# SwiGLU block of a two-layer encoder trunk: block products in two PSUM banks, scratch tiles taken out, and loads of the down stretch placed elsewhere

## The chip, the cores and the metric

One core of a Trainium2 chip runs the whole program in one launch. The metric is the device time of that launch in microseconds (us). TensorE (PE in the profile) does matmuls, VectorE (DVE), ScalarE (ACT) and GpSimd (POOL) do elementwise work, and SyncE (SP) issues nearly all DMA transfers from one queue, in order.

## The reference

Two layers work on x of 1024 tokens by 1024 channels in float32. Each layer has a mixing half (windowed attention, spatial gating, a convolution) and then the block that is changed here, followed by a gated projection of a side input p (1024 by 256 for each layer):

```
h = RMSNorm(x) * g_ffn
x = x + (silu(h @ w_gate) * (h @ w_up)) @ w_down        # w_gate_up: 1024 x 5632, w_down: 2816 x 1024
x = x + (p[i] @ w_ple_proj) * sigmoid(RMSNorm(x) @ w_ple_gate)
```

## The kernel before, in words

**Layout and precision.** Activations lie with channels in the 128 partitions and tokens along the free axis, in two halves of 512 tokens (`HALF`, `hf`). Every float32 operand is split in two parts, `wh`/`wl` for weights and the two halves of an `hl` or `tf` tile for activations. One step of a product (`step_mm`, L224, L226, L228) is then three matmuls of 128x128 by 128x512. ScalarE makes the first part of a split (`copy_h`, L122), VectorE the second (`sub_l`, L125 and L216). `load_w` (L211 to L216) loads a weight tile into one of three `raw` slots and splits it into one of three `wh` and three `wl` slots.

**Where tiles live.** `U` gives one of 38 tiles of 1024 floats, `T` one of 6 scratch tiles of 512 floats (tags `s`, `sg`, `ws`, `cu`, `t1`, `u2`, `g`, `ac`, `st`, `sq` and others all share these six). PSUM has eight banks of 128x512: three behind `BA` (`pa`), four behind `BT` (`pt`), one behind `BO` (`po`). `BU` alternates between `BT` and `BA`. The order of the instructions on each engine is not the order of the code: a scheduler in the framework lays them out, and inserts a wait where a slot or a bank has to come free first.

**Gate and up products.** The 2816 inner channels are worked as 11 pairs `j` of 2x128. For a pair, gate (`i`=0) and up (`i`=1) are 2x2 block products over two halves of the 1024 channels, done with seven block products in place of eight. `first(j)` (L1118) does the two block products that belong to token half 0 and the first 128 channels of the pair: for `k`=0..3 into a bank, VectorE saves that partial sum times the norm's row `bc` in `s1` (L1131) which goes to DRAM (`sum_d`, L1132), then `k`=4..7 go on in the same bank, and the finished bank is multiplied (L1137), passed through silu (L1138), multiplied on GpSimd (L1139), and for up multiplied into the result (L1141), which goes to `act_d`. `rest(j)` (L1172) does the other five products for gate and for up, 60 matmuls each: GpSimd makes sums of weight blocks (L1216 to L1220; the first, `s3`, in a scratch tile `ws`), ScalarE and VectorE split them (`wform`), the products go to three banks, and VectorE adds them up (L1224, L1226) and ends them (`out_of`: L1208 and silu L1209 for gate; L1212 into a scratch tile `cu` and then L1213 for up). The results go to `act_d` (L1233, L1234).

**Order.** `first(0)` to `first(4)` run while the mixing half still runs (the ahead stage; there all banks come from `BA` and the weight parts are cast on VectorE, L215, and subtracted on GpSimd). Then the second token half is finished (`wo_second(1)`), `token_forms` (L1156) normalises x (`normed`, L1153) and makes the token sums and their splits, `first(5)` to `first(7)` follow (with the forms: the token-form stage), then `rest(0)` to `rest(10)`, with one of `first(8)` to `first(10)` behind each of `rest(0)` to `rest(2)`. From `rest(3)` on no first is left; these are called steady rests here.

**Down stretch.** The side input p is loaded into `raw` slots and transposed (L1262, L1267), `w_ple_proj` as well (L1275). Then for each token half: x is loaded (L1285), and for the 22 tiles of 128 inner channels a `w_down` tile (L211) and an activation tile `ac` in a scratch slot (L1291) are loaded, split, and multiplied into all eight banks; L1299 adds x and `norm_add` starts the next norm.

## Time and profile before

| | us |
|---|---|
| median of 3 runs | 2665.69 |
| lowest and highest of them | 2662.81, 2669.3 |
| the profiled execution | 2667.72 |
| its span in the trace | 2665.9 |
| mean granted clock of TensorE | 0.952 of full speed |

The profile is one execution, 2.0 us slower than the median. Times in rows count from the start of the span. "Idle before" is how long the engine stood still before an instruction, with the instruction that released it. The rows are of layer 1; layer 2 has the same sequence.

### The profile page before, as it was taken

The page shows a single profiled execution, that of the slowest core. Times are in us where ns is not written, and L with a number is a line of the kernel's source. Part 1 is how long each engine was busy: PE and PEld are TensorE (multiplying, and loading weights), DVE is VectorE, ACT ScalarE, POOL GpSimd, SP SyncE. Part 2 cuts the span into 40 slices and gives each one's busy share as a digit, 9 for nine tenths or more (in the row PEclk, how much of TensorE's full clock was granted, in tenths as well). Part 3 has the DMA queues.
Part 4 walks back from the last instruction along what each step waited for, and adds up shares of the span by engine and source line. Part 5 has one row for each costly group of instructions (what it writes and reads, how often), then busy time and mean ns, then how long its engine had stood idle before and what let it go on. Part 6 is the DMA issues. An engine that isn't in the chain of part 4 may idle for free. (4 is left out here: it accounts for less than half of the span.)

```text
span 2665.9 us, 30234 instructions
## 1 busy us (share of the span) xinstructions
PE 2387.9 (90%) x11404; PEld 1972.8 (74%) x11404; DVE 1453.5 (55%) x2241; ACT 905.5 (34%) x1610; POOL 744.6 (28%) x551
## 2 busy tenths in 40 slices
PE   8898889688988889899999898896898888898999
PEld 6897767567766668688789876675776666786887
DVE  6986674644544452525469567646444444526252
ACT  5246661312222241424323457412212222424142
POOL 5123345532332300103421233464323333001031
PEclk9999998899999989899999999898999999999999
DMA  6011324333333262523321031344333332625332
GB/s 205 24 52 56 119 84 161 118 124 113 131 103 103 87 217 95 198 95 107 96 71 37 33 111 64 126 150 123 123 111 99 103 103 87 241 95 197 95 99 67
DMA packets 243346, 294.78 MB, mean 111 GB/s; under 512 B 11348, under 2 KB 180912, under 8 KB 243200
## 3 DMA queue, kind: packets, MB, share of 16 engines
q1 hardware_dynamic: 236704, 283.16, 32.4%
q10 hardware_dynamic: 6016, 9.45, 1.1%
q8 instruction: 90, 1.47, 0.2%
q0 software_dynamic: 480, 0.24, 0.1%
q14 instruction: 56, 0.46, 0.1%
HBM read 228.84 MB, written 63.96 MB: 110 GB/s over the span
## 5 line engine op out<-in xcount | busy, mean ns | idle before, releaser
L216 DVE TENSOR_TENSOR wl<-raw,wh 128x1024 fp32r<-128x1024 f32 x172 | 218.9, 1273 | 337.5 <-ACT wh L122 327.7
L224 PE MATMUL pt<-tf,wh 128*128 128x512 f32 x792 | 326.5, 415 | 54.7 <-ACT wh L122 54.7
L122 ACT ACTIVATE wh<-raw 128x1024 fp32r<-128x1024 f32 x172 | 182.0, 1059 | 532.2 <-PE pt L226 376.9
L226 PE MATMUL pt<-tf,wh 128*128 128x512 f32 x792 | 323.3, 408 | 0.0
L224 PE MATMUL pa<-hl,wh 128*128 128x512 f32 x648 | 264.4, 409 | 62.9 <-DVE s L1131 52.9
L228 PE MATMUL pt<-tf,wl 128*128 128x512 f32 x792 | 315.4, 404 | 0.0
L224 PE MATMUL pa<-tf,wh 128*128 128x512 f32 x704 | 280.0, 400 | 19.5 <-ACT wh L122 19.5
L264 POOL TENSOR_TENSOR st<-st,sq 128x512 f32<-128x512 f32 x82 | 123.4, 1506 | 610.2 <-ACT sq L263 607.9
L228 PE MATMUL pa<-tf,wl 128*128 128x512 f32 x704 | 273.1, 394 | 9.2 <-DVE wl L125 9.2
L226 PE MATMUL pa<-tf,wh 128*128 128x512 f32 x704 | 277.0, 394 | 0.0
L228 PE MATMUL pa<-hl,wl 128*128 128x512 f32 x648 | 259.1, 404 | 4.5 <-POOL wl L216 3.3
L226 PE MATMUL pa<-hl,wh 128*128 128x512 f32 x648 | 262.1, 405 | 1.0 <-DVE hl L128 0.8
L224 PEld LDWEIGHTS pt<-tf,wh 128*128 128x128 f32 x792 | 159.4, 201 | 98.4 <-ACT wh L122 64.0
L1216 POOL TENSOR_TENSOR ws<-rw,rw 128x512 f32<-128x512 f32 x44 | 63.7, 1448 | 511.5 <-DVE cu L1212 337.6
L224 PEld LDWEIGHTS pa<-hl,wh 128*128 128x128 f32 x648 | 125.8, 194 | 99.6 <-DVE s L1131 59.3
L607 PE MATMUL pa<-wh,hl 128*128 128x256 f32 x640 | 181.1, 288 | 16.4 <-ACT zkv L620 11.7
L226 PEld LDWEIGHTS pt<-tf,wh 128*128 128x128 f32 x792 | 157.6, 199 | 33.9
L228 PEld LDWEIGHTS pt<-tf,wl 128*128 128x128 f32 x792 | 156.3, 197 | 34.2
L609 PE MATMUL pa<-wl,hl 128*128 128x256 f32 x640 | 181.6, 286 | 0.0
L610 PE MATMUL pa<-wh,hl 128*128 128x256 f32 x640 | 180.8, 286 | 0.0
L224 PEld LDWEIGHTS pa<-tf,wh 128*128 128x128 f32 x704 | 134.9, 192 | 55.7 <-ACT wh L122 28.8
L122 ACT ACTIVATE wh<-rw 128x512 fp32r<-128x512 f32 x176 | 102.6, 618 | 208.2 <-POOL rw L1218 172.8
(309 smaller groups left out, 4933.9 us busy)
## 6 DMA issues: line engine op xcount, KB each, us to landing
rw<-in_w_gate_up_dram SPq DMA_DIRECT2D x88, 512.0 KB, 6.0
raw<-in_w_down_dram SPq DMA_DIRECT2D x88, 512.0 KB, 3.6
raw<-in_w_gate_up_dram SPq DMA_DIRECT2D x44, 512.0 KB, 4.5
ac<-act SPq DMA_DIRECT2D x88, 256.0 KB, 5.0
raw<-in_w_ple_gate_dram SPq DMA_DIRECT2D x32, 512.0 KB, 4.1
raw<-in_w_in_dram SPq DMA_DIRECT2D x28, 512.0 KB, 3.8
raw<-in_w_out_dram SPq DMA_DIRECT2D x24, 512.0 KB, 3.7
sum<-s SPq DMA_DIRECT2D x44, 256.0 KB, 2.2
```

The source lines that it names most:

```text
L122: nc.scalar.activation(dst, src, AF.Copy, scale=scale)
L216: (eng or nc.vector).tensor_tensor(out=l, in0=raw, in1=f(h), op=ALU.subtract)
L224: nc.tensor.matmul(b, lhsT=wh, rhs=hl[:, 0:512], start=first, stop=False, skip_group_check=again)
L226: nc.tensor.matmul(b, lhsT=wh, rhs=hl[:, 512:1024], start=False, stop=False, skip_group_check=again)
L228: nc.tensor.matmul(b, lhsT=wl, rhs=hl[:, 0:512], start=False, stop=last, skip_group_check=again)
L264: (eng or nc.gpsimd).tensor_tensor(out=n.s, in0=n.s, in1=sq, op=ALU.add)
L607: nc.tensor.matmul(o, lhsT=x_[:, th], rhs=wh, start=(kc + k == 0), stop=False)
L609: nc.tensor.matmul(o, lhsT=x_[:, th], rhs=wl, start=False, stop=False)
L610: nc.tensor.matmul(o, lhsT=x_[:, tl], rhs=wh, start=False, stop=(kc == 1 and k == 3))
L1216: tt(out=s3, in0=a21, in1=a22, op=ALU.add)
```

## The change

In `first`, both weight tiles are loaded ahead of the products, and each product's two halves go to two banks instead of one (from `BA` in the ahead stage, otherwise from `BU`). The first bank gives `s1` (L1137 of the changed kernel), the second is multiplied by `bc` in place, in PSUM (L1140), `s1` is added (L1141), and silu (L1143) and the product of gate and up (L1144) follow; the multiply on GpSimd is gone. In `rest`, the weight sum `s3` takes the free half of the result tile `ga`, and the tile `cu` is replaced by work in place in the bank (L1213, L1214) or in `g` (L1231, L1232). p is loaded early into `U` tiles, `w_ple_proj` during tile 8 and x during tile 12 of the down stretch, and `ac` takes a `U` tile.

```diff
--- before.py
+++ after.py
@@ -1119,27 +1119,30 @@
 
             hl0, bc = nrm[0].hl, nrm[0].bc
             c0 = 2 * j * P
-            a = None
-            for i, off in enumerate((0, DFF)):
-                wh, wl = load_w(rows_of(w_gate_up[layer], 0, NK, off + c0, P), (NK, P),
-                                nc.gpsimd if ahead else None, nc.vector if ahead else None)
-                b = BA()
-                for k in range(NK):
-                    step_mm(b, (wh[:, k, :], wl[:, k, :]), hl0[k], k == 0, k % HK == HK - 1, True)
-                    if k == HK - 1:
-                        s1 = T("s1")
+            ws = [load_w(rows_of(w_gate_up[layer], 0, NK, off + c0, P), (NK, P),
+                         nc.gpsimd if ahead else None, nc.vector if ahead else None)
+                  for off in (0, DFF)]
+            a = T("sg")
+            for i, (wh, wl) in enumerate(ws):
+                bank = BA if ahead else BU
+                s1 = T("s1")
+                for h in range(2):
+                    b = bank()
+                    for k in range(h * HK, (h + 1) * HK):
+                        step_mm(b, (wh[:, k, :], wl[:, k, :]), hl0[k], k % HK == 0,
+                                k % HK == HK - 1)
+                        if k % 2 == 1:
+                            bg.tick()
+                    if h == 0:
                         nc.vector.tensor_tensor(out=s1, in0=b, in1=bc, op=ALU.mult)
                         nc.sync.dma_start(out=sum_d[j][i], in_=s1)
-                    if k % 2 == 1:
-                        bg.tick()
+                    else:
+                        nc.vector.tensor_tensor(out=b, in0=b, in1=bc, op=ALU.mult)
+                        nc.vector.tensor_tensor(out=b if i else a, in0=b, in1=s1, op=ALU.add)
                 if i == 0:
-                    a = T("sg")
-                    nc.vector.tensor_tensor(out=a, in0=b, in1=bc, op=ALU.mult)
                     nc.scalar.activation(a, a, AF.Silu)
-                    nc.gpsimd.tensor_tensor(out=a, in0=a, in1=bc, op=ALU.mult)
-                else:
-                    nc.vector.tensor_tensor(out=a, in0=b, in1=a, op=ALU.mult)
-                    nc.sync.dma_start(out=act_d[2 * j][:, HALF[0]], in_=a)
+            nc.vector.tensor_tensor(out=a, in0=b, in1=a, op=ALU.mult)
+            nc.sync.dma_start(out=act_d[2 * j][:, HALF[0]], in_=a)
 
         forms = [[None] * HK for _ in range(5)]
 
@@ -1182,8 +1185,7 @@
                                                               off + 2 * j * P, 2 * P))
                 a11, a21, a12, a22 = (raw[h][:, :, c * P:(c + 1) * P] for h in range(2)
                                       for c in range(2))
-                sm = T("ws")
-                s3 = sm.rearrange("p (k m) -> p k m", k=HK)
+                s3 = ga[:, 0:512].rearrange("p (k m) -> p k m", k=HK)
                 tt = nc.gpsimd.tensor_tensor
                 pool_w = []
 
@@ -1208,13 +1210,11 @@
                         nc.vector.tensor_tensor(out=dst, in0=b, in1=src, op=ALU.add)
                         nc.scalar.activation(dst, dst, AF.Silu)
                     else:
-                        c = T("cu")
-                        nc.vector.tensor_tensor(out=c, in0=b, in1=src, op=ALU.add)
-                        nc.vector.tensor_tensor(out=dst, in0=c, in1=dst, op=ALU.mult)
+                        nc.vector.tensor_tensor(out=b, in0=b, in1=src, op=ALU.add)
+                        nc.vector.tensor_tensor(out=dst, in0=b, in1=dst, op=ALU.mult)
 
                 bank = BT if i else BA
                 tt(out=s3, in0=a21, in1=a22, op=ALU.add)
-                w22 = None
                 tt(out=a21, in0=a11, in1=a21, op=ALU.subtract)
                 tt(out=a11, in0=s3, in1=a11, op=ALU.subtract)
                 tt(out=a12, in0=a12, in1=a11, op=ALU.subtract)
@@ -1225,7 +1225,12 @@
                 prod(bd, wform(a21), 1, True, True)
                 nc.vector.tensor_tensor(out=g, in0=bd, in1=u2, op=ALU.add)
                 prod(bc_, wform(s3), 2, True, True)
-                out_of(gb[:, 512:1024], g, bc_)
+                if i == 0:
+                    out_of(gb[:, 512:1024], g, bc_)
+                else:
+                    nc.vector.tensor_tensor(out=g, in0=bc_, in1=g, op=ALU.add)
+                    nc.vector.tensor_tensor(out=gb[:, 512:1024], in0=g, in1=gb[:, 512:1024],
+                                            op=ALU.mult)
                 prod(bd, wform(a22), 3, False, True)
                 out_of(gb[:, 0:512], u2, bd)
                 prod(bc_, wform(a12), 4, False, True)
@@ -1255,44 +1260,50 @@
                 first(AHEAD + 1 + BEHIND + j)
 
 
+        pin = [U("pin").rearrange("p (b m) -> p b m", b=4) for _ in range(2)]
+        for hf in range(2):
+            nc.sync.dma_start(out=pin[hf], in_=p[layer, 0, hf * 512:(hf + 1) * 512, :]
+                              .rearrange("(b q) m -> q b m", q=P))
...
         pw = []
-        for c in range(2):
-            raw = wp.tile([P, 1024], F32, tag="raw", name=nm("praw"))
-            nc.sync.dma_start(out=raw, in_=w_ple_proj[layer, c * P:(c + 1) * P, :])
-            ph, pl = U("pwh", F32R), U("pwl", F32R)
-            copy_h(ph, raw)
-            sub_l(pl, raw, ph)
-            pw.append((ph, pl))
+
+        def proj_weights():
+            for c in range(2):
+                raw = U("praw")
+                nc.sync.dma_start(out=raw, in_=w_ple_proj[layer, c * P:(c + 1) * P, :])
+                ph, pl = U("pwh", F32R), U("pwl", F32R)
+                copy_h(ph, raw)
+                sub_l(pl, raw, ph)
+                pw.append((ph, pl))
+
 
         nx = [None, None]
         for hf in range(2):
-            xps = [U("X").rearrange("p (m s) -> p m s", m=2) for _ in range(4)]
-            for mp in range(4):
-                nc.sync.dma_start(out=xps[mp], in_=xd[2 * mp:2 * mp + 2, :, HALF[hf]]
-                                  .rearrange("m p s -> p m s"))
             banks = [BO()] + [BA() for _ in range(3)] + [BT() for _ in range(4)]
             for fi in range(NF):
                 wh, wl = load_w(rows_of(w_down[layer], fi * P, 1, 0, D), (1, D))
-                t = T("ac")
+                t = U("ac")[:, 0:512]
                 nc.sync.dma_start(out=t, in_=act_d[fi][:, HALF[hf]])
                 a = split(t)
                 for m in range(NK):
                     cs = slice(m * P, (m + 1) * P)
                     step_mm(banks[m], (wh[:, 0, cs], wl[:, 0, cs]), a, fi == 0, fi == NF - 1)
+                if fi == 8 and hf == 0:
+                    proj_weights()
+                if fi == 12:
+                    xps = [U("X").rearrange("p (m s) -> p m s", m=2) for _ in range(4)]
+                    for mp in range(4):
+                        nc.sync.dma_start(out=xps[mp], in_=xd[2 * mp:2 * mp + 2, :, HALF[hf]]
+                                          .rearrange("m p s -> p m s"))
             nx[hf] = Norm()
             for m in range(NK):
                 xo = X[hf][m] = xps[m // 2][:, m % 2]
```

**VectorE in the ahead stage of layer 1**, where the row `st_2511` of the first norm becomes known (`pa` are the banks of the firsts, X the tiles of x that L1153 or L1156 normalise). Before, behind L1131 for `pa_4065` and seven of the eight L1153:

```order
L1153 SCALAR_TENSOR_TENSOR X_3790<-X_3790,cols_189,st_2511 128x512
L215 CAST wh_4172<-raw_4171 128x1024
L1137 TENSOR_TENSOR sg_4093<-pa_4065,st_2511 128x512
L1131 TENSOR_TENSOR s_680_4116<-pa_4103,st_2511 128x512
L1131 TENSOR_TENSOR s_685_4152<-pa_4139,st_2511 128x512
L215 CAST wh_4208<-raw_4207 128x1024
L1141 TENSOR_TENSOR sg_4093<-pa_4103,sg_4093 128x512
```

Now, behind L1137 for `pa_4073`, four of the eight L1156 and a cast:

```order
L1156 SCALAR_TENSOR_TENSOR X_3788<-X_3788,cols_189,st_2511 128x512
L1140 TENSOR_TENSOR pa_4088<-pa_4088,st_2511 128x512
L1156 SCALAR_TENSOR_TENSOR X_3790<-X_3790,cols_189,st_2511 128x512
L1156 SCALAR_TENSOR_TENSOR X_3788<-X_3788,cols_189,st_2511 128x512
L1156 SCALAR_TENSOR_TENSOR X_3790<-X_3790,cols_189,st_2511 128x512
L215 CAST wh_4216<-raw_4215 128x1024
L1140 TENSOR_TENSOR pa_4120<-pa_4120,st_2511 128x512
L1141 TENSOR_TENSOR sg_4071<-pa_4088,s_677_4072 128x512
L1137 TENSOR_TENSOR s_680_4104<-pa_4105,st_2511 128x512
L1141 TENSOR_TENSOR pa_4120<-pa_4120,s_680_4104 128x512
```

The banks' evacuations went from three in a row behind the eighth normalisation to five, spread between normalisations and casts; the bank `pa_4088` comes free with the L1141 near the end of this piece.

**GpSimd in the steady rests** (`rw` are the weight blocks of one `i`; the lower-numbered pair of `rw` is loaded first). Before, the up part of one pair and the gate of the next:

```order
L1216 TENSOR_TENSOR ws_6297<-rw_6293,rw_6294 128x512
L1218 TENSOR_TENSOR rw_6293<-rw_6293 128x4x128
L1219 TENSOR_TENSOR rw_6293<-ws_6297,rw_6293 128x4x128
L1220 TENSOR_TENSOR rw_6294<-rw_6294,rw_6293 128x4x128
L1216 TENSOR_TENSOR ws_6404<-rw_6400,rw_6401 128x512
L1218 TENSOR_TENSOR rw_6400<-rw_6400 128x4x128
L1219 TENSOR_TENSOR rw_6400<-ws_6404,rw_6400 128x4x128
L1220 TENSOR_TENSOR rw_6401<-rw_6401,rw_6400 128x4x128
```

Now, the same two parts:

```order
L1217 TENSOR_TENSOR ga_6208<-rw_6311,rw_6312 128x512
L1218 TENSOR_TENSOR rw_6311<-rw_6311 128x4x128
L1219 TENSOR_TENSOR rw_6311<-ga_6208,rw_6311 128x4x128
L1217 TENSOR_TENSOR ga_6410<-rw_6414,rw_6415 128x512
L1220 TENSOR_TENSOR rw_6312<-rw_6312,rw_6311 128x4x128
L1218 TENSOR_TENSOR rw_6414<-rw_6414 128x4x128
L1219 TENSOR_TENSOR rw_6414<-ga_6410,rw_6414 128x4x128
L1220 TENSOR_TENSOR rw_6415<-rw_6415,rw_6414 128x4x128
```

The first weight sum of the next gate (into `ga_6410`) stands ahead of the last one of the running up part; the sum goes to `ga`, not to a scratch tile `ws`.

TensorE at the same place (`pt` are the banks of the up part, `pa` those of the next gate). Before, the gate's first matmuls stand behind the fifth, last up product:

```order
L226 MATMUL pt_5890<-tf_4707,wh_5961 128x512
L228 MATMUL pt_5890<-tf_4707,wl_5962 128x512
L224 MATMUL pa_5995<-tf_4622,wh_5998 128x512
L226 MATMUL pa_5995<-tf_4622,wh_5998 128x512
L224 MATMUL pa_5996<-tf_4625,wh_5998 128x512
L226 MATMUL pa_5996<-tf_4625,wh_5998 128x512
```

Now 14 of the gate's 60 matmuls (12 into `pa_6018`, 2 into `pa_6019`) stand behind the third up product, and the fourth and fifth follow them:

```order
L228 MATMUL pt_5917<-tf_4721,wl_5953 128x512
L224 MATMUL pa_6018<-tf_4642,wh_6021 128x512
L226 MATMUL pa_6018<-tf_4642,wh_6021 128x512
L224 MATMUL pa_6019<-tf_4645,wh_6021 128x512
L226 MATMUL pa_6019<-tf_4645,wh_6021 128x512
L228 MATMUL pa_6018<-tf_4642,wl_6022 128x512
L224 MATMUL pa_6018<-tf_4666,wh_6021 128x512
```

Of the gate, 46 matmuls are left behind the last up product.

**SP ahead of the down stretch of layer 1** (`rw` and `act` belong to the last two rests, `ac` and `raw_7...<-in_w_down` to the down stretch). Before:

```order
L1234 DMA act_118<-gb_7225 128x1024
L1291 DMA ac_7501<-act_97 128x512
L211 DMA raw_7495<-in_w_down_dram 128x1024
L1291 DMA ac_7536<-act_98 128x512
L1291 DMA ac_7571<-act_99 128x512
L1233 DMA act_117<-ga_7224 128x512
L1291 DMA ac_7606<-act_100 128x512
L1291 DMA ac_7641<-act_101 128x512
L1285 DMA X_7479<-xd 128x2x512
```

Now:

```order
L1265 DMA pin_7420<-in_p_dram 128x4x256
L1265 DMA pin_7421<-in_p_dram 128x4x256
L1295 DMA ac_7470<-act_97 128x512
L1295 DMA ac_7505<-act_98 128x512
L1295 DMA ac_7540<-act_99 128x512
L211 DMA raw_7569<-in_w_down_dram 128x1024
L1295 DMA ac_7575<-act_100 128x512
L1295 DMA ac_7610<-act_101 128x512
L1295 DMA ac_7645<-act_102 128x512
L1239 DMA act_118<-gb_7219 128x1024
L211 DMA raw_7604<-in_w_down_dram 128x1024
```

Three `w_down` tiles (`raw_7464`, `raw_7499`, `raw_7534`) stand some 65 to 78 places further up in the queue, between the rests, and six `ac` loads ahead of the last rest's results; x is not in this piece any more, and p is where `w_ple_proj` was.

## Rows read from the trace of the kernel before

**Rows 1.** The page's first part: engine, busy time in us (share of the span), instructions.

```profile
PE 2387.9 (90%) x11404; PEld 1972.8 (74%) x11404; DVE 1453.5 (55%) x2241; ACT 905.5 (34%) x1610; POOL 744.6 (28%) x551
```

**Rows 2.** The waits of PE over the whole span: engine, first letters of the tile it was to write, its line, then whom it waited for; us in total, times, longest in us.

```profile
PE pt L224 <- ACT wh L122: 54.7, 22, 2.5
PE pa L224 <- DVE s L1131: 52.9, 14, 10.9
PE po L224 <- ACT tf L122: 31.1, 4, 8.8
```

**Rows 3.** Layer 1 in stretches (us from the span's start): busy us of PE, PEld, DVE, ACT, POOL with the number of instructions, granted clock as a share of full speed, DMA share, GB/s.

```profile
497.00:540.00 43.00, 21.20 (x66) 15.87 (x67) 40.12 (x47) 15.24 (x26) 17.52 (x10) 0.68 0.26 84
552.30:690.00 137.70, 123.79 (x513) 98.99 (x514) 67.67 (x90) 31.42 (x51) 37.69 (x28) 0.96 0.36 117
690.00:957.50 267.50, 236.43 (x965) 187.23 (x964) 126.39 (x182) 57.44 (x102) 83.18 (x60) 0.95 0.29 97
957.50:985.00 27.50, 18.32 (x65) 14.30 (x64) 17.09 (x21) 14.06 (x19) 0.00 (x0) 0.81 1.02 368
```

**Rows 4.** The ahead stage of layer 1 in order of time, PE, ACT and DVE: start us, us, engine, line, operation, tiles, xcount, [idle before <-releaser].

```profile
409.19 0.63 PE L226 MATMUL pa<-hl,wh 128*128 128x512 f32 x1
409.62 0.63 PE L228 MATMUL pa<-hl,wl 128*128 128x512 f32 x1
411.27 1.11 PE L281 MATMUL pt<-ident,rcol 128*128 128x128 f32 x4 [0.17 <-POOL rcol L270]
420.36 0.50 PE L224 MATMUL pa<-hl,wh 128*128 128x512 f32 x1 [1.01 <-DVE sg L1137]
...
412.42 0.58 ACT L298 COPY st<-pt 128x512 f32<-128x512 f32 x1 [2.88 <-PE pt L281]
...
413.11 0.69 DVE L1131 TENSOR_TENSOR s<-pa,st 128x512 f32<-128x512 f32 x1 [0.78 <-ACT st L298]
413.72 5.38 DVE L1153 SCALAR_TENSOR_TENSOR X<-X,cols,st 128x512 f32<-128x512 f32 x8
```

**Rows 5.** The token-form stage of layer 1, PE in order of time (columns as in rows 4).

```profile
505.89 0.80 PE L224 MATMUL pa<-hl,wh 128*128 128x512 f32 x1 [9.11 <-DVE s L1131]
548.45 0.50 PE L224 MATMUL pa<-hl,wh 128*128 128x512 f32 x1 [1.38 <-DVE s L1131]
552.31 0.50 PE L224 MATMUL pa<-tf,wh 128*128 128x512 f32 x1 [0.84 <-ACT wh L122]
```

**Rows 6.** One cycle of the steady rests of layer 1 (columns as in rows 4): PE, DVE, ACT, POOL, SP.

```profile
717.80 0.39 PE L228 MATMUL pt<-tf,wl 128*128 128x512 f32 x1
719.12 0.50 PE L224 MATMUL pa<-tf,wh 128*128 128x512 f32 x1 [0.94 <-ACT wh L122]
720.97 0.51 PE L228 MATMUL pa<-tf,wl 128*128 128x512 f32 x1 [0.65 <-DVE wl L125]
721.32 0.40 PE L224 MATMUL pa<-tf,wh 128*128 128x512 f32 x1
733.57 0.39 PE L228 MATMUL pa<-tf,wl 128*128 128x512 f32 x1
736.45 0.50 PE L224 MATMUL pt<-tf,wh 128*128 128x512 f32 x1 [2.49 <-ACT wh L122]
752.92 0.50 PE L224 MATMUL pa<-tf,wh 128*128 128x512 f32 x1 [0.94 <-ACT wh L122]
...
718.23 0.69 DVE L1212 TENSOR_TENSOR cu<-pt,u 128x512 f32<-128x512 f32 x1 [0.96 <-PE pt L228]
718.95 1.36 DVE L1213 TENSOR_TENSOR ga<-cu,ga 128x512 f32<-128x512 f32 x1
...
734.73 0.63 ACT L1209 ACTIVATE ga<-ga 128x512 f32<-128x512 f32 x1 [2.09 <-DVE ga L1208]
...
713.56 1.79 POOL L1216 TENSOR_TENSOR ws<-rw,rw 128x512 f32<-128x512 f32 x1 [13.32 <-DVE cu L1212]
727.94 1.29 POOL L1216 TENSOR_TENSOR ws<-rw,rw 128x512 f32<-128x512 f32 x1 [8.17 <-DMA rw<-in_w_gate_up_dram]
730.68 1.29 POOL L1219 TENSOR_TENSOR rw<-ws,rw 128x512 f32<-128x512 f32 x1
...
720.34 0.32 SPq L1233 DMA_DIRECT2D act<-ga  x1
721.23 2.05 SPq L1181 DMA_DIRECT2D rw<-in_w_gate_up_dram  x4
```

**Rows 7.** The start of the down stretch of layer 1: PE, then SP.

```profile
965.10 0.79 PE L224 MATMUL po<-tf,wh 128*128 128x512 f32 x1 [6.94 <-ACT tf L122]
975.14 0.50 PE L224 MATMUL po<-tf,wh 128*128 128x512 f32 x1 [2.23 <-ACT wh L122]
...
961.31 3.56 SPq L1285 DMA_DIRECT2D X<-xd  x4
965.23 1.65 SPq L211 DMA_DIRECT2D raw<-in_w_down_dram  x3
```

**Rows 8.** The change of halves in the down stretch of layer 1: PE, then ACT.

```profile
1100.12 0.79 PE L224 MATMUL po<-tf,wh 128*128 128x512 f32 x1 [8.83 <-ACT tf L122]
...
1099.43 1.92 ACT L122 ACTIVATE tf<-ac 128x512 fp32r<-128x512 f32 x3 [1.43 <-DMA ac<-act]
```

**Rows 9.** Groups of instructions over the whole span: line, engine, operation, tiles, shapes, xcount | busy us, mean ns of one | idle us before them and releaser.

```profile
L1213 DVE TENSOR_TENSOR ga<-cu,ga 128x512 f32<-128x512 f32 x22 | 29.3, 1332 | 0.5
L1131 DVE TENSOR_TENSOR s<-pa,st 128x512 f32<-128x512 f32 x44 | 29.7, 683 | 17.9 <-PE pa L228 15.7 <-ACT st L298 2.2
L1139 POOL TENSOR_TENSOR sg<-sg,st 128x512 f32<-128x512 f32 x22 | 30.2, 1372 | 55.4 <-ACT sg L1138 46.4 <-issue 9.0
```

8 lines of the change are left out of this document (2 added, 6 removed).

## The prediction, made before the changed kernel ran

> **What bounds the kernel now.** I read the busy times first: TensorE works 2387.9 us of the span, 90% [rows 1]; no other engine is above 55%. A change of the order can therefore only win TensorE's idle time or its time at low clock, and the question is where in the FFN these lie. The waits of TensorE answer it [rows 2]: 52.9 us for L1131, that is for VectorE to read a half-done bank in `first`; 54.7 us for a weight split in `rest`'s up part, 22 times and at most 2.5 us; 31.1 us for an activation split in the down stretch, in four waits. The stretches [rows 3] then say who is behind each wait. From 497 to 540 VectorE is busy 40.1 of 43 us and TensorE 21.2: there VectorE is the bound. In the steady rests (690 to 957.5) TensorE is busy 236 of 267 us and VectorE not half of it, so the idle time is that of a chain. From 957.5 to 985 the DMA engines are full (share 1.02), at 368 GB/s, with a granted clock of 0.81.
>
> Two steps recur. At full clock the sixth and the last of a gate's 60 matmuls start at 721.32 and 733.57 [rows 6]: 54 steps of 0.227 us. At half clock two start 0.43 us apart [rows 4] (409.19 and 409.62). The two levels are 2.4 and 1.2 GHz.
>
> **The change part by part**, for one layer; both layers have the same sequence.
>
> *First, operations.* VectorE did four operations in a `first` and now does seven; with 0.683 us for a product out of PSUM [rows 9] three more are 2.07 us, and over 22 firsts 66 x 0.69 = 45.5 us. GpSimd loses 22 multiplies of 1.37 us, 30.2 us [rows 9], which TensorE never waited for: nothing. Writing into a PSUM bank from VectorE is in no row. The nearest are 0.69 us for PSUM in and SBUF out and 1.33 us for two SBUF operands [rows 9]; I take 0.69, because one operand and the length are the same, and keep 1.33 for the range.
>
> *Ahead stage: +8 us (+4 to +11).* Before, the row `bc` was made by transposes at 411.27, was in SBUF at 413.0, and TensorE began the 49th matmul of the products ahead at 420.36, behind 1.01 us of waiting for L1137 [rows 4]. In the new order the transposes stand behind some 10 matmuls more, at half clock 4.3 us or more: I estimate 415.5 to 417, `bc` ready near 418. TensorE's 49th matmul then needs the bank `pa_4088` (only three `BA` banks take turns). VectorE's order puts ahead of that bank's last read L1137, eight L1156 (5.38 us for eight), two casts, two L1140 and L1141: 0.69 + 5.4 + 1.4 + 1.4 + 0.7, with overlaps some 9.3 us. That is 427.3 in place of 420.36, 7 us, and about 1 us more until the clock is up. Low end: the transposes come first after all. High end: 1.33 us for the work in PSUM.
>
> *Token-form stage: -6 us (-9 to 0).* The waits of 9.1 and up to 10.9 us for L1131 go [rows 2, 5], but VectorE is 93% busy there and gets three firsts more work, 6.2 us. The forms would be done near 540 + 6.2; before, `rest(0)` began at 552.31 after the firsts' left matmuls [rows 5], which in the new order have been done under cover of VectorE's work. So `rest(0)` starts at 546 or so. If VectorE's line of work lengthens all of it, nothing is won.
>
> *Firsts between rests: -6.5 us (-8 to -3).* Each of three has a wait for L1131 of 1.38 us and one of 0.84 us for the next weight split [rows 5]: 2.2 x 3. VectorE, 67.7 busy of 137.7 us [rows 3], covers 2.07 us more.
>
> *Steady rests: -7 us (-15 to +3).* A cycle takes 33.80 us, 719.12 to 752.92, with 120 matmuls (27.2 us), waits of 0.94, 0.65 and 2.49 us, and 2.5 us for the clock and short waits [rows 6]. The first two waits come from GpSimd: L1216 stood 13.32 us for the scratch slot of `cu`, and started the gate's weights only at 713.56. Without the scratch tile they are ready early, and 14 gate matmuls run ahead of the last two up products. The third wait stays, in another form. Before, the up part's weights were ready (L1219 done at 731.97) while ScalarE held their copy behind the silu at 734.73. Now let E be the end of the last up product (before, the matmul at 717.80 ends at 718.2). Only 46 gate matmuls follow, 10.4 us. The up weights' loads are issued by SP behind the `act` write, and that behind L1213: before at 721.23, E + 3.0. With the multiply at 0.69 in place of 1.36 us it is E + 2.4. From issue to L1216 took 6.7 us (727.94), three sums to the end of L1219 take 4.0, ScalarE's copy 0.63: TensorE goes on at about E + 13.8. So a wait of 3.4 us takes the place of all three; then 74 matmuls (16.8 us) and about 2.2 us of low clock and short waits: 32.8 us, 1.0 less, in seven transitions. Best: the wait stays at 2.5 us and the clock falls less. Worst: the multiply takes 1.36 us and the longer wait costs a second stretch at half clock.
>
> The length of that multiply is a row: 1.36 us with two SBUF operands beside GpSimd's work, 0.69 us for the operation out of PSUM [rows 6]. The Trainium skill, page "GPSIMD Engine Reference", section "1. Specifications", says that GpSimd's SBUF interfaces are shared with VectorE, with contention when a VectorE instruction has two SBUF inputs; by it the multiply, with one operand in PSUM now, would not stretch even if GpSimd ran beside it. By the rule the sum stands; by the old row kept, the cycle would be 33.5 us and this term -2 us.
>
> *Start of the down stretch: -12.5 us (-13.3 to -9).* Of 957.5 to 985, 27.5 us, TensorE needs 60 matmuls or 13.6 us; some 13.3 us are lost, in waits of 6.94 and 2.23 us and at low clock [rows 3, 7]. SP issued four x loads from 961.31, 2 MB, and only then three `w_down` tiles, at 965.23. In the new order three tiles stand between the rests, six `ac` loads ahead of the last results, x and `w_ple_proj` at tiles that run inside a stretch of unbroken matmuls with free DMA; TensorE starts tiles 0 and 1 among the last up products. What is late next is `act` of the last pair, needed only by tiles 20 and 21. I leave 0.8 us for the clock.
>
> *Change of halves: -1.2 us (-1.5 to +1).* The wait of 8.83 us ends with a split of `ac` at 1099.43, of which 1.43 us was for the load behind a scratch slot [rows 8]; before that ScalarE and VectorE work on the next norm, which stays.
>
> Sum: +8 - 6 - 6.5 - 7 - 12.5 - 1.2 = -25.2, twice -50.4. The profiled execution took 2667.7 us, 2.0 us above the median of the runs, so 2617 from the one and 2615 from the other: I say **2616**. Taking the half-widths as independent, about 12 us a layer, this case's own range is 2593 to 2639.
>
> **The rivals.**
>
> *VectorE takes it back (slower).* VectorE has 45.5 us of added work, all of it in firsts. If in every first its last operation on a bank ends later than TensorE wants the bank, the 45.5 us lie on the path and the firsts win nothing. It decides where VectorE's work in a stretch passes TensorE's. Against it: this is so from 497 to 540, but not in the firsts between rests [rows 3]. With steady rests unchanged and the down stretch as forecast: 2667.7 + 45.5 - 27.4 = 2686.
>
> *The steady rests win nothing.* The chain through SP and the loads is longer than worked out, or costs a second stretch at half clock: 2616 + 14 = 2630. For it: the loads of four tiles need 6.7 us from issue to use, whatever slots are free [rows 6].
>
> *Separate banks help ahead too.* If VectorE reads the banks between normalisations early enough, TensorE gets over the 7 us and the old 1.01 us: 2616 - 2 x 9 = 2598. Against it: three banks and the order on VectorE. The Trainium skill, page "Perfetto Trace Analysis", section "Matmuls", advises to rotate independent products through different banks so that the evacuation of one overlaps the next; by it this stage would gain. The trace so far speaks for it in the token-form stage alone, where the bank was reread.
>
> *The change doesn't do what it says.* The early tiles land but the activation splits still come late, behind ScalarE's and VectorE's work for the last rest or for want of `U` tiles, and the down stretch starts as before: 2616 + 25 = 2641.
>
> **How the numbers follow.** The forecast 0.50, VectorE taking it back 0.05, steady rests without gain 0.22, gain ahead 0.15, down stretch as before 0.08. The three rivals on the faster side lie at 2630, 2598 and 2641; the range from 2592 to 2648 takes them in with some of their spread, and leaves out the slower rival and the tails. A measurement of this kernel can tell some 0.2%, 5 us, from no change. Slower by more than that is the first rival, 0.05; within it 0.03, from the steady and down rivals together with a bad ahead stage; faster 0.92.
>
> **What would show it.** Right: the 49th matmul ahead starts near 427 rather than 420; no wait of 9 to 11 us from 497 to 540 and `rest` starts 6 us sooner against the stretch's start; cycles of 32.8 us with a single wait of 3 to 4 us at the up part, ended by ScalarE's copy behind L1219; full clock across the start of the down stretch with no x load there. Wrong: an added operation in PSUM far from 0.69 us; TensorE waiting for L1141 or L1144 in the firsts between rests; the wait at the up part at 2.5 us or above 5; a wait of over 3 us at the first tiles of the down stretch.

## The result, and the profile after

The changed kernel took 2600.9 us (median of 4 runs, 2595.1 to 2605.9), the kernel before 2664.5 us in the same runs: ratio 0.976, 95% interval 0.973 to 0.978. The gain of some 64 us is on the forecast's side, and the time lies inside its range (2592 to 2648); the forecast was 2616, a gain of some 50.

The page's first part for the changed kernel, to be read against [rows 1]:

```profile
PE 2359.6 (91%) x11404; PEld 1969.8 (76%) x11404; DVE 1555.2 (60%) x2307; ACT 916.3 (35%) x1610; POOL 735.6 (28%) x529
```

TensorE's busy time fell by 28 us although it does the same 11404 instructions, so on average they ran shorter. VectorE took on 102 us in 66 instructions more, far over the 45.5 us of 66 x 0.69. Most of the rest is in the splits of the weight blocks, one group of which is, before and then now (columns as in rows 9):

```profile
L125 DVE TENSOR_TENSOR wl<-rw,wh 128x512 fp32r<-128x512 f32 x176 | 123.5, 738 | 31.8 <-ACT wh L122 31.8
L125 DVE TENSOR_TENSOR wl<-rw,wh 128x512 fp32r<-128x512 f32 x176 | 187.0, 1076 | 30.8 <-ACT wh L122 28.7
```

The same 176 splits take 63 us more. GpSimd's weight sums now run beside many of them, which the last section comes back to; in the steady cycles of layer 1 TensorE has no wait for a split by VectorE. Who TensorE waited for (columns as in rows 2):

```profile
PE pt L224 <- ACT wh L122: 64.2, 22, 4.3
PE pa L224 <- DVE sg L1141: 33.1, 4, 11.4
PE po L224 <- ACT tf L122: 14.6, 2, 7.3
PE pa L224 <- DVE s L1137: 10.5, 5, 7.3
```

The waits for L1131 [rows 2] went from 52.9 us to 33.1 + 10.5 us for two other lines; those for `ac` halved; those at the up part grew from 54.7 to 64.2 us, now without the gate's waits of 0.94 and 0.65 us [rows 6] beside them. Stretches of the changed kernel (columns as in rows 3): from the up part of `rest(0)` to that of `rest(3)`, on to that of `rest(10)`, then from there into the down stretch:

```profile
573.14:698.76 125.62, 118.17 (x504) 96.58 (x505) 76.71 (x97) 30.69 (x49) 34.05 (x25) 0.97 0.39 128
698.76:924.28 225.52, 202.83 (x852) 164.60 (x852) 136.51 (x164) 54.30 (x93) 82.48 (x56) 0.95 0.32 109
924.28:957.00 32.72, 32.72 (x146) 27.10 (x147) 24.26 (x31) 16.28 (x23) 0.99 (x1) 1.00 0.53 185
```

and of the kernel before, the first two between the same matmuls:

```profile
568.73:704.29 135.56, 121.66 (x504) 97.23 (x504) 65.55 (x88) 29.89 (x49) 37.05 (x27) 0.96 0.36 117
704.29:940.81 236.52, 207.93 (x841) 164.11 (x841) 112.91 (x162) 51.26 (x92) 78.01 (x56) 0.95 0.29 97
940.81:985.00 44.19, 35.01 (x136) 27.99 (x137) 25.69 (x35) 17.25 (x25) 0.00 (x0) 0.85 0.68 243
```

The last line of each is the clearest: a stretch with 35.0 us of work in 44.2 at a clock of 0.85 became unbroken work at full clock. Its two ends are not the same matmul; it holds 120 matmuls and 16 transposes of p before, 142 and 4 now. The other 12 transposes now fill the last wait of the middle line. In the middle line idle time fell from 28.6 to 22.7 us and busy time from 207.9 to 202.8.

**Ahead stage**, TensorE and VectorE in order of time (columns as in rows 4):

```profile
415.77 0.60 PE L281 MATMUL pt<-ident,rcol 128*128 128x128 f32 x4
428.22 0.80 PE L224 MATMUL pa<-hl,wh 128*128 128x512 f32 x1 [7.37 <-DVE sg L1141]
...
417.10 0.69 DVE L1137 TENSOR_TENSOR s<-pa,st 128x512 f32<-128x512 f32 x1 [4.70 <-ACT st L298]
420.29 3.49 DVE L1156 SCALAR_TENSOR_TENSOR X<-X,cols,st 128x512 f32<-128x512 f32 x2
423.71 0.69 DVE L1140 TENSOR_TENSOR pa<-pa,st 128x512 f32<-128x512 f32 x1
427.49 0.68 DVE L1141 TENSOR_TENSOR sg<-pa,s 128x512 f32<-128x512 f32 x1
```

The transposes stand at 415.77 in place of 411.27, the 49th matmul at 428.22 in place of 420.36 [rows 4]; it waits 7.37 us for L1141, which ends at 428.17 behind normalisations and casts. One of the two normalisations at 420.29 took 2.8 us, beside a 2.7 us subtraction on GpSimd; the other seven took 0.74 each. The operation in place in PSUM (L1140) takes 0.69 us.

**Token-form stage**, TensorE, then VectorE:

```profile
528.14 0.80 PE L224 MATMUL pa<-hl,wh 128*128 128x512 f32 x1 [6.96 <-DVE sg L1141]
549.17 0.79 PE L224 MATMUL pa<-hl,wh 128*128 128x512 f32 x1 [11.43 <-DVE sg L1141]
...
545.57 2.35 DVE L125 TENSOR_TENSOR tf<-X,tf 128x512 fp32r<-128x512 f32 x2
547.84 0.69 DVE L1140 TENSOR_TENSOR pt<-pt,st 128x512 f32<-128x512 f32 x1
548.44 0.67 DVE L1141 TENSOR_TENSOR sg<-pa,s 128x512 f32<-128x512 f32 x1
```

TensorE still waits twice, 7.0 and 11.4 us, now for L1141 behind VectorE's token sums and splits; before, the two waits were 9.1 and 10.9 us. So they fell by 1.6 us only. What is gone are four short waits behind them, 1.1, 0.8, 1.4 and 0.8 us; two of 0.4 and 1.2 us are new. VectorE works without a gap from 507.4 until the second L1141 ends at 549.1.

**A cycle of the steady rests**: TensorE, VectorE, GpSimd, SP:

```profile
715.48 0.39 PE L228 MATMUL pt<-tf,wl 128*128 128x512 f32 x1
725.91 0.39 PE L228 MATMUL pa<-tf,wl 128*128 128x512 f32 x1
729.49 0.50 PE L224 MATMUL pt<-tf,wh 128*128 128x512 f32 x1 [3.19 <-ACT wh L122]
...
715.91 0.70 DVE L1213 TENSOR_TENSOR pt<-pt,u 128x512 f32<-128x512 f32 x1 [0.23 <-PE pt L228]
717.11 0.69 DVE L1214 TENSOR_TENSOR ga<-pt,ga 128x512 f32<-128x512 f32 x1
...
724.78 1.29 POOL L1217 TENSOR_TENSOR ga<-rw,rw 128x512 f32<-128x512 f32 x1 [20.65 <-DMA rw<-in_w_gate_up_dram]
727.50 1.27 POOL L1219 TENSOR_TENSOR rw<-ga,rw 128x512 f32<-128x512 f32 x1
...
717.83 0.32 SPq L1238 DMA_DIRECT2D act<-ga  x1
718.72 2.06 SPq L1184 DMA_DIRECT2D rw<-in_w_gate_up_dram  x4
```

The last up product's last matmul starts at 715.48 and ends near 715.87 (E); the `act` write is at E + 2.0, the loads at E + 2.9, the first weight sum at E + 8.9, the third ends at E + 12.9, TensorE goes on at E + 13.6. The gate's waits are gone. Over the seven cycles of the stretch TensorE goes on between E + 13.6 and E + 14.6, on the mean E + 13.9.

**The change of halves**:

```profile
1065.65 0.80 PE L224 MATMUL po<-tf,wh 128*128 128x512 f32 x1 [7.30 <-ACT tf L122]
1071.75 0.50 PE L226 MATMUL po<-tf,wh 128*128 128x512 f32 x1 [2.36 <-DVE tf L125]
```

Before, the second wait was this one:

```profile
1104.67 0.80 PE L226 MATMUL po<-tf,wh 128*128 128x512 f32 x1 [0.78 <-DVE tf L125]
```

The first wait is 7.30 in place of 8.83 us [rows 8], the second, for VectorE's part of the split, 2.36 in place of 0.78. Together they are 9.66 us, and were 9.61: nothing is won here.

Five stages of layer 1, in us, for the kernels below, each from TensorE's start of one instruction to that of the next: 1 from the last transposes of the mixing half (near 402) to those of the second norm (near 496), 2 to the up part of `rest(0)`, 3 to that of `rest(3)`, 4 to that of `rest(10)`, 5 to the second half of the down stretch, so that the second wait at the change of halves comes after it. Starts are read from TensorE's rows in order of time.

| kernel | 1 | 2 | 3 | 4 | 5 |
|---|---|---|---|---|---|
| before | 93.6 | 72.6 | 135.6 | 236.5 | 159.3 |
| changed | 103.5 | 67.1 | 125.6 | 225.5 | 141.4 |
| down stretch alone | 95.1 | 72.6 | 134.0 | 237.8 | 141.9 |
| firsts alone | 102.1 | 65.1 | 126.7 | 236.5 | 157.2 |
| rests alone | 95.1 | 71.7 | 130.3 | 226.1 | 154.9 |
| one bank | 95.1 | 72.7 | 130.3 | 229.3 | 141.9 |
| BU ahead | 94.8 | 66.2 | 124.3 | 226.4 | 141.8 |
| act writes on ScalarE | 102.1 | 66.3 | 124.2 | 214.8 | 141.4 |
| cu back | 103.5 | 67.1 | 125.6 | 226.1 | 141.4 |
| ws back | 102.3 | 65.1 | 126.6 | 216.8 | 141.4 |

The two layers of one execution differ by up to some 3.6 us in a stage, in stage 4 of one bank and cu back by 5; a difference below that in this table shows nothing by itself.

### The profile page after: what moved, and what is told of

It is laid out like the page before. It is cut to its first block, busy times and chain, and to the rows that moved or that the text cites. A ratio compares the mean times of both kernels' runs of the same rounds, so it can differ in the third digit from the quotient of the medians.

```text
span 2600.5 us, 30145 instructions
## 1 busy us (share of the span) xinstructions
PE 2359.6 (91%) x11404; PEld 1969.8 (76%) x11404; DVE 1555.2 (60%) x2307; ACT 916.3 (35%) x1610; POOL 735.6 (28%) x529
## 5 line engine op out<-in xcount | busy, mean ns | idle before, releaser
L224 PE MATMUL pt<-tf,wh 128*128 128x512 f32 x792 | 322.5, 409 | 64.2 <-ACT wh L122 64.2
L226 PE MATMUL pt<-tf,wh 128*128 128x512 f32 x792 | 320.3, 404 | 0.0
L224 PE MATMUL pa<-hl,wh 128*128 128x512 f32 x564 | 232.5, 413 | 48.3 <-DVE sg L1141 33.1
L226 PE MATMUL pa<-tf,wh 128*128 128x512 f32 x704 | 274.9, 391 | 0.0
L224 PE MATMUL pa<-tf,wh 128*128 128x512 f32 x704 | 273.8, 391 | 0.0
L226 PE MATMUL pa<-hl,wh 128*128 128x512 f32 x564 | 229.3, 407 | 0.9 <-DVE hl L128 0.8
L228 PE MATMUL pa<-hl,wl 128*128 128x512 f32 x564 | 227.1, 403 | 0.0
L1217 POOL TENSOR_TENSOR ga<-rw,rw 128x512 f32<-128x512 f32 x44 | 64.2, 1460 | 519.1 <-DMA rw<-in_w_gate_up_dram 510.6
L125 DVE TENSOR_TENSOR wl<-rw,wh 128x512 fp32r<-128x512 f32 x176 | 187.0, 1076 | 30.8 <-ACT wh L122 28.7
L224 PEld LDWEIGHTS pa<-hl,wh 128*128 128x128 f32 x564 | 111.6, 198 | 77.0 <-DVE sg L1141 34.8
```

What stands on the lines that cost most here:

```text
L125: nc.vector.tensor_tensor(out=dst, in0=src, in1=f(h), op=ALU.subtract)
L224: nc.tensor.matmul(b, lhsT=wh, rhs=hl[:, 0:512], start=first, stop=False, skip_group_check=again)
L226: nc.tensor.matmul(b, lhsT=wh, rhs=hl[:, 512:1024], start=False, stop=False, skip_group_check=again)
L228: nc.tensor.matmul(b, lhsT=wl, rhs=hl[:, 0:512], start=False, stop=last, skip_group_check=again)
L1217: tt(out=s3, in0=a21, in1=a22, op=ALU.add)
```

## The experiments

Ratios are to the kernel before, run beside each, with 95% intervals.

**Down stretch alone** (`down_only`): the kernel before with the last part of the diff, from `pin` to the x loads, and no more.

> The kernel before with the change's down stretch alone (p, w_ple_proj, x and ac as in the change; firsts and rests as before). Theory A, the loads were what the start of the down stretch waited for: from the last up part to the tenth tile some 17 us a layer go, as in the changed kernel, so about 2664 - 34 = 2630 us, and the waits of 6.9 and 2.2 us are gone. Rival: the start was covered only because the rests' last up products no longer wait for scratch slots; then the first split of ac stays behind VectorE's and ScalarE's work of the last rest, only half goes, about 2647 us, with a wait over 3 us at the first tiles.

2631.0 us, ratio 0.987 (0.984 to 0.991). Theory A holds: stage 5 shrank by 17.4 us with the rests untouched, and the waits of 6.9 and 2.2 us are gone.

**Firsts alone** (`firsts_only`): the kernel before with the changed `first()`.

> The kernel before with the change's first() alone (two banks, both weights loaded ahead). Theory A, read stage by stage from the changed kernel: ahead stage +9 us, token-form stage -5, three firsts between rests -1.4 each, in sum about nothing: 2660 to 2668 us. Rival 1, VectorE takes it back: the 66 added operations, 45 us, lie on the path: about 2700 us. Rival 2, separate banks win everywhere: 2640 us or less, without a wait of 7 us at the 49th matmul ahead.

2649.8 us, ratio 0.994 (0.993 to 0.996). Rival 1 falls; VectorE's work is covered. Rival 2 falls too, since the 49th matmul waits here as well:

```profile
PE pa L224 <- DVE sg L1141: 42.0, 6, 7.4
```

But theory A's 2660 to 2668 us was missed, too: stage 3 shrank by 8.9 us alone, where I had read 4.2 as this edit's share.

**Rests alone** (`rest_only`): the kernel before with the changed `rest()`.

> The kernel before with the change's rest() alone (weight sum in ga, work in place in the bank, no scratch tiles ws and cu). Theory A: the cycle of the steady rests goes from 33.8 to 32.2 us, the waits for the gate's weights (0.94, 0.65, and 0.77 behind the firsts) go, the wait at the up part grows from 2.5 to 3.5: 11 us a layer and some 2 to 6 behind firsts, about 2664 - 28 = 2636 us. Rival: the gate's weights could be early only because GpSimd lost its multiply in first and the firsts' banks were free; then the wait at the up part takes back what the others give and the time is 2655 to 2664 us.

2631.2 us, ratio 0.989 (0.986 to 0.991): near theory A's 2636. Stage 4 shrank by 10.4 us. Something else showed in its waits:

```profile
PE pt L224 <- ACT wh L122: 76.7, 22, 4.7
PE pa L224 <- DVE s L1131: 40.6, 6, 9.7
```

The waits for L1131 fell from 14 to 6 [rows 2] although `first()` still works in one bank. The gate's weights of the next rest are ready early here too, and TensorE has other matmuls while VectorE reads the bank. So this edit and the two banks cover the same waits.

**One bank** (`one_bank`): the changed kernel with one bank in `first()`, both weights still loaded ahead:

```diff
-                for h in range(2):
-                    b = bank()
...
+                b = BA()
+                for k in range(NK):
+                    step_mm(b, (wh[:, k, :], wl[:, k, :]), hl0[k], k == 0, k % HK == HK - 1, True)
```

> The changed kernel with first() working in one bank again (multiply on GpSimd too), but with both weight tiles still loaded ahead of the products. Theory A, the banks alone matter in first: the 49th matmul ahead is back near 420 us (-9 us a layer), waits of about 9 us for L1131 return in the token-form stage (+5) and of 1.4 us behind each of three firsts (+4): 2598 to 2606 us, about the same as the changed kernel's 2601. Rival, the loads ahead made the gain of the token-form stage and the firsts: those waits stay away and the time is 2580 to 2590 us.

2605.6 us, ratio 0.979 (0.976 to 0.983), not apart from the changed kernel's. The time is theory A's, and the 49th matmul and the token-form waits came back as it said (stages 1 and 2); the 1.4 us behind the firsts did not, for the reason just told; in their place the up part waits 3.3 to 4.3 us in stage 3, where the changed kernel waits 2.5. So beside the other two edits the two banks win nothing that these runs can tell: of what they give in stages 2 and 3, 10 us in layer 1, stage 1 takes back 8.4.

The three parts alone give 35, 16 and 35 us, 85 in all (34.8 + 16.0 + 34.6), together 64. The table says where the difference went: over layer 1 stage 3 gives 1.6 + 8.9 + 5.3 alone and 10.0 together, stage 5 gives 17.4 + 2.1 + 4.4 alone and 17.9 together; that is some 12 us a layer won by more than one part alone. In stage 3 both `firsts_only` and `rest_only` take the waits for L1131. In stage 5 `rest_only` shortens the two waits at the first down tiles from 6.94 and 2.23 to 5.48 and 1.33 us, and the down stretch's own edit removes them.

**BU ahead** (`bu_ahead`): `bank = BU` in `first()` in all stages.

> The changed kernel with the banks of the ahead stage taken from BU as well, seven banks in turn in place of three. Theory A, TensorE stood 7.4 us at the 49th matmul because one of three banks had to be read first: that wait goes, the second norm's transposes come 8 to 9 us sooner in each layer, in sum 2601 - 17 = 2584 us. Rival, VectorE's line of normalisations, casts and bank reads sets the end of the ahead stage: the wait only moves to a later matmul and the time is 2596 to 2606 us.

2577.7 us, ratio 0.967 (0.965 to 0.968): theory A, and 6 us below its 2584. From 402 to 498 TensorE has three waits of 0.3 us or more (TensorE in order of time):

```profile
402.39 1.11 PE L281 MATMUL pt<-ident,ar 128*128 128x128 f32 x4 [3.88 <-POOL ar L270]
406.33 1.87 PE L292 MATMUL po<-ones,st 128*128 128x1 f32 x8 [2.83 <-POOL st L264]
...
497.15 0.65 PE L281 MATMUL pt<-ident,rcol 128*128 128x128 f32 x4 [0.30 <-POOL rcol L270]
```

No wait is left between the first norm at 406 and the second, and stage 1 is back at 94.8 us. VectorE's backlog of normalisations and casts is the same; with seven banks TensorE is not held by it.

**Act writes on ScalarE** (`act_q`): in `rest()`

```diff
-            nc.sync.dma_start(out=act_d[2 * j][:, HALF[1]], in_=ga[:, 512:1024])
-            nc.sync.dma_start(out=act_d[2 * j + 1], in_=gb)
+            nc.scalar.dma_start(out=act_d[2 * j][:, HALF[1]], in_=ga[:, 512:1024])
+            nc.scalar.dma_start(out=act_d[2 * j + 1], in_=gb)
```

> The changed kernel with the two act writes of each rest issued by ScalarE in place of SP, so that the weight blocks' loads no longer stand behind them in SP's queue. Theory A, the wait at the up part hangs on the chain end of the last up product, act write, loads, three sums, copy: the loads are issued about 1 us or more sooner, the wait falls from 3.5 to the 2.5 us that ScalarE's silu sets, 14 us in all: 2587 us. Rival 1, the loads wait for their U tiles, not for the queue: issue time, wait and total as in the changed kernel, 2601 us. Rival 2, the writes now hold up ScalarE's splits: over 2605 us.

2576.0 us, ratio 0.966 (0.965 to 0.968). Theory A, and more than it said (2587). The order on TensorE is the changed kernel's, with 14 gate matmuls ahead and 46 behind. TensorE, GpSimd and SP in a cycle whose last up product ends at 712.8:

```profile
725.74 0.80 PE L224 MATMUL pt<-tf,wh 128*128 128x512 f32 x1 [2.48 <-ACT wh L122]
...
711.52 1.29 POOL L1217 TENSOR_TENSOR ga<-rw,rw 128x512 f32<-128x512 f32 x1 [10.49 <-DVE wl L125]
...
703.23 2.03 SPq L1184 DMA_DIRECT2D rw<-in_w_gate_up_dram  x4
```

The loads are issued at 703.23, not 1 but 12 us sooner against E; GpSimd's sum then waits for a reader of its tile and no more for a load. The wait at the up part is 2.48 us, where ScalarE's silu stands ahead of the copies. Beside the changed kernel stage 4 shrank by 10.8 us, of which idle time is 6.3 (22.7 to 16.4) and the rest is busy time: 852 instructions in 198.3 in place of 202.8 us.

**cu back** (`cu_back`): the up part's `c = T("cu")` and its multiply from SBUF again.

> The changed kernel with the scratch tile cu back in the up part's first two ends (weight sum still in ga), so that the multiply has two SBUF operands again. Theory A, the multiply took 1.36 us because GpSimd worked beside it, and GpSimd now idles there: 0.69 us again with two SBUF operands, cycle 32.2 us, total 2598 to 2604. Rival, two SBUF operands cost 1.33 us by themselves: act write, loads and the up part's start 0.65 us later in 14 cycles, 2610 us.

2594.0 us, ratio 0.973 (0.971 to 0.974), somewhat under theory A's 2598 to 2604 and not clearly apart from the changed kernel. Theory A holds; the groups of the two multiplies over the span:

```profile
L1215 DVE TENSOR_TENSOR gb<-cu,gb 128x512 f32<-128x512 f32 x22 | 15.1, 688 | 0.2
L1215 DVE TENSOR_TENSOR ga<-cu,ga 128x512 f32<-128x512 f32 x22 | 15.1, 686 | 0.0
```

0.69 us with two SBUF operands, where [rows 9] had 1.33: GpSimd stands idle during all 44 of them now. In the kernel before, 20 of the 22 multiplies of [rows 9] ran beside GpSimd's work and took 1.36 to 1.46 us, and the two that did not took 0.69. So the place of the operand in PSUM is not what made this multiply shorter here. The Trainium skill, page "GPSIMD Engine Reference", section "1. Specifications", has contention for VectorE instructions with two SBUF inputs; this run agrees, in that the stretching is gone (0.69 us) where GpSimd idles.

**More VectorE work** (`more_dve`): L1140 a second time.

> The changed kernel with L1140 done twice (the second multiplication by the norm's row is extra and changes the result), 44 more VectorE operations of 0.69 us in the firsts, 30 us. Theory A, VectorE is on the path in the ahead stage's first norm and the token-form stage alone: about 1.4 and 4 us a layer, nothing in the firsts between rests: 2608 to 2616 us. Rival, VectorE is on the path in every first: 2625 to 2632 us.

2605.5 us, ratio 0.978 (0.976 to 0.980): 4.6 us above the changed kernel for 30 us of added work, with overlapping intervals. The rival falls; theory A's 2608 to 2616 was missed, too, by 2.5 us. The 49th matmul's wait grew by 1.2 us, near the 1.4 that theory A had,

```profile
429.47 0.80 PE L224 MATMUL pa<-hl,wh 128*128 128x512 f32 x1 [8.56 <-DVE sg L1142]
```

but the token-form stage, where theory A had 4 us, did not get longer in layer 1 (66.6 us beside 67.1). One of the added operations fell into a gap of VectorE, and the order was another: the last L1140 ahead of the long wait's L1141 now stands behind it. Whether that stage is VectorE's alone stays open.

**ws back** (`ws_back`): the changed kernel with the weight sum in scratch again:

```diff
-                s3 = ga[:, 0:512].rearrange("p (k m) -> p k m", k=HK)
+                s3 = T("ws").rearrange("p (k m) -> p k m", k=HK)
```

> The changed kernel with the weight sum of rest() in a scratch tile ws again, cu still gone. Theory A, the gate's first weight sum was late because ws had to wait until a scratch tile came free at the end of the last up product: the waits of 0.94 and 0.65 us come back, cycle near 33.8 us, and with the firsts behind rests some 12 us a layer: about 2625 us. Rival, cu was what held the six scratch tiles; without it a slot for ws is free in time and the cycle stays at 32.2 us, total 2595 to 2605.

2579.7 us, ratio 0.968 (0.967 to 0.970). Theory A (2625) was wrong, and the kernel is 21 us faster than the changed one. Without `cu` the scratch slot is free in time, so the rival's premise held, but the gain has another source. TensorE, GpSimd and SP in a cycle whose last up product ends at 716.2:

```profile
729.38 0.39 PE L228 MATMUL pa<-tf,wl 128*128 128x512 f32 x1
732.25 0.60 PE L224 MATMUL pt<-tf,wh 128*128 128x512 f32 x1 [2.48 <-ACT wh L122]
...
725.56 1.29 POOL L1217 TENSOR_TENSOR ws<-rw,rw 128x512 f32<-128x512 f32 x1 [20.14 <-DMA rw<-in_w_gate_up_dram]
728.30 1.29 POOL L1219 TENSOR_TENSOR rw<-ws,rw 128x512 f32<-128x512 f32 x1
...
719.24 2.10 SPq L1184 DMA_DIRECT2D rw<-in_w_gate_up_dram  x4
```

The loads come at E + 3.1 and the sums at E + 9.4, no sooner than in the changed kernel. But here the order leaves all 60 gate matmuls behind the last up product, and they last until 729.77, E + 13.6, when the up part's weights are ready but for ScalarE's silu: a wait of 2.48 us. In the changed kernel 14 of them had been put ahead, the 46 left ended at E + 10.4, and TensorE waited 3.2 to 4.1 us for the same chain in the six cycles in which no transposes fill the wait. In stage 4 of layer 1 the kernel with both scratch tiles takes 236.5 us (`firsts_only`), with `cu` alone 226.1 (`cu_back`), with `ws` alone 216.8 (`ws_back`), with neither 225.5. Either tile's going makes the gate's weights early; `ws`' going besides brings the order that moves the 14 matmuls, and costs about half of what `cu`'s going alone wins.

**Both, and a third edit** (`both`, `both_early`, `ws_early`). `both` is `bu_ahead` with `act_q`. `both_early` also writes the first three tiles of the second half ahead of the first half's additions:

```diff
+            if hf == 0:
+                early += [operands(1, fi) for fi in range(3)]
             nx[hf] = Norm()
...
-                a = split(t)
+                (wh, wl), a = early.pop(0) if early else operands(hf, fi)
```

where `operands` holds the lines that load and split a tile. `ws_early` has `ws_back` in place of `act_q`.

> The changed kernel with seven banks in turn in the ahead stage and the rests' act writes issued by ScalarE, the edits of bu_ahead and act_q together. Theory A, they act on different stages and add up: 2601 - 23 - 25 = 2553 us, waits at the up part 2.48 us, no wait of 7 us at the 49th matmul. Rival, part of one is taken back by the other: over 2560 us.

> As both, and the loads and splits of the second token half's first three tiles in the down stretch are written ahead of the first half's additions and norm, so that ScalarE and VectorE do them first. Theory A, the wait of 7.3 us at the change of halves hangs on ScalarE's copy of ac behind eight norm inputs: what is left is the reading of the banks, 1 to 2 us, with less low clock: about 8 us a layer, 2553 - 16 = 2537 us. Rival, TensorE's banks come free only as VectorE reads all eight behind the norm's work: the wait is spread over several matmuls and under 6 us in all are won, 2547 us or more.

> As both_early, but with the weight sum in the scratch tile ws again in place of ScalarE issuing the act writes (SP issues them as in the changed kernel). The two edits are two ways to the same 1 us in each cycle: one has the loads issued sooner, the other leaves all 60 gate matmuls behind the last up product as cover. Theory A: waits at the up part 2.48 us again, cycles 30.0 to 31.6 us, total as both_early, 2524 to 2536 us. Rival, in ws_back the gain came from the token-form stage with three banks (wait of 6.2 in place of 11.4 us), which seven banks have already: the up part waits 3 us and more again, about 2550 us.

`both`: 2553.2 us, ratio 0.958 (0.957 to 0.960), additive as theory A said. `both_early`: 2529.0 us, ratio 0.950 (0.947 to 0.952), 24 us less, where theory A had 16; the stretch from the last up part over the change of halves (columns as in rows 3):

```profile
902.40:1070.00 167.60, 167.59 (x743) 138.78 (x744) 86.09 (x100) 67.79 (x91) 10.92 (x7) 1.00 0.52 174
```

167.6 us of unbroken work at full clock: no wait for a bank or a split is left at the change of halves. `ws_early`: 2538.0 us beside 2670.7 for the kernel before, ratio 0.950 (0.947 to 0.952), the same ratio; its waits at the up part are 2.48 us again. The two edits are two ways to the same time.

## Why the prediction was right, and where its sizes were off

By the steps of the prediction, for one layer, forecast and measured (layer 1, stages of the table; the 17.9 us of stage 5 are parted by the change of its first wait at the change of halves, 1.5 us, which the second wait takes back):

| step | forecast | measured |
|---|---|---|
| ahead stage | +8 | +9.9 |
| token-form stage | -6 | -5.5 |
| firsts between rests | -6.5 | -9.9 |
| steady rests | -7 | -11.0 |
| start of the down stretch | -12.5 | -16.4 |
| change of halves | -1.2 | 0 |

The measured steps add up to -32.9, twice -65.8; the two profiled executions are 65.4 us apart. The forecast's sum was -25.2.

*Ahead stage*: right in mechanism. The bank `pa_4088` came free at 428.2, forecast 427.3, and `bu_ahead` shows that it was the number of banks. That the two times lie so close is in part luck: `bc` was ready near 417.1 and not 418, and VectorE's line to that bank took 11.1 us and not 9.3, mainly for the one long normalisation.

*Token-form stage*: right in size, but not in all of the mechanism. The prediction had the waits of 9.1 and 10.9 us go and named a wait of 9 to 11 us as a sign that must be missing; waits of 7.0 and 11.4 us came, for L1141. The firsts' left matmuls were done under cover, as it said, and the waits behind them went. It called VectorE the bound; in the trace VectorE has no gap up to the end of the long wait, but `more_dve` did not lengthen the stage, so this is not shown by experiment.

*Firsts*: the waits were as listed; what the term left out is shorter work. Of 9.9 us, idle time is 6.5 (135.56 - 121.66 to 125.62 - 118.17), and 3.5 us is the same 504 matmuls running shorter, in part by the clock: one of the three rests ran wholly at full clock (38.4 us for its 168 matmuls, before 40.4 at a clock of 0.965). And the cover was double: `rest_only` shows that either edit takes these waits.

*Steady rests*: the chain was right (E + 13.6 in the cycle shown, E + 13.9 on the mean, forecast E + 13.8), and `act_q` shows that it hangs on SP's queue. Mis-sized were the low clock and the short waits, forecast 2.2 us a cycle: 32.2 us a cycle measured less 13.9 and 16.8 leave 1.5. Three of the seven cycles ran at full clock in 30.7 to 31.6 us, three at 0.90 to 0.93 in 32.7 to 33.8. One step of the reasoning was wrong though the sum was not: the prediction took the longer wait of 3.4 us as the price of early weights. `ws_back` shows that `cu`'s going alone makes the weights early without that price, and that the moved matmuls are lost cover, 1.2 us a cycle. For the multiply 0.69 us was the right value; `cu_back` shows that it would have been so with two SBUF operands as well, as GpSimd idles there.

*Down stretch*: `down_only` shows the mechanism at its start. The prediction began to count the loss at 957.5; but the 16.7 us before, from 940.81, already held 3.1 us beyond 60 matmuls at full clock, at a granted clock of 0.90 and with 12 of the 16 transposes of p, which now run in the wait ahead of them. The change of halves was wrong: the load no longer holds `ac` up, but VectorE's part of the split takes the gain back.

*GpSimd and VectorE*: the prediction put GpSimd's change at nothing and VectorE's at 45.5 us. VectorE took on 102, as GpSimd's sums came to stand beside its splits. `firsts_only` and `more_dve` show that added work of VectorE is mostly covered; what these longer splits cost by themselves no run shows.

*Rivals*: "VectorE takes it back" fell with `firsts_only` and `more_dve`. "Separate banks help ahead too" was false with three banks. With seven the loss is gone: stage 1 takes 94.8 and 91.1 us in the two layers of `bu_ahead`, before 93.6 and 94.3, so no gain over one bank is clear of the scatter. The Trainium skill (page "Perfetto Trace Analysis", section "Matmuls") advises to rotate independent products through different banks so that the evacuation of one overlaps the next; here that took seven banks, and with three stage 1 was 9.9 us longer than before. The other two rivals fell, as the steady rests and the down stretch won.

## What to carry to other kernels

Bring work forward only if it is not the cover of a longer chain behind it: find the chain that starts at the end of a cycle (here write, load, three sums, copy) and count the matmuls that run over it. Either shorten the chain (`act_q`) or leave it its cover (`ws_back`). When two edits remove waits of one stage, time them apart and together; the sum of the parts said 85 us, the whole 64. A wait can cost more than its length, as with the cycles at 0.90 to 0.93 of the clock above, so read busy time at equal instruction counts beside idle time.

## What the runs showed of the hardware that was not expected

VectorE's operations on two SBUF operands, 0.68 to 0.69 us by themselves, mostly took about twice as long beside GpSimd's work. The multiply takes 0.69 us while GpSimd idles; it took 1.33 us on the mean of the 22 of [rows 9], 20 of them beside GpSimd's work. The changed kernel shows it within one cycle, by two splits of the same form, the first beside two of GpSimd's sums and the second without any (VectorE, then GpSimd):

```profile
701.21 1.77 DVE L125 TENSOR_TENSOR wl<-ga,wh 128x512 fp32r<-128x512 f32 x1
713.80 0.68 DVE L125 TENSOR_TENSOR wl<-ga,wh 128x512 fp32r<-128x512 f32 x1
...
700.81 1.62 POOL L1219 TENSOR_TENSOR rw<-ga,rw 128x512 f32<-128x512 f32 x1
702.51 1.62 POOL L1220 TENSOR_TENSOR rw<-rw,rw 128x512 f32<-128x512 f32 x1
```

GpSimd's sums are longer too, 1.62 us here and 1.27 at 727.50. Of the 176 splits `wl<-rw`, 95 have no GpSimd work beside them and take 0.68 us each; 67 lie wholly beside it and take 1.54 on the mean.

VectorE's operation in place in PSUM, for which no row stood, takes 0.69 to 0.70 us, like one that writes to SBUF. It has one operand in PSUM and does not stretch: 10 of the 44 L1140 lie wholly beside GpSimd's work, and they too take 0.69 us.
